# Reordered attention and mixer steps, stage results handed on by feature halves, first weights in two transfers

## The chip, the core and the metric

One kernel runs on one core of a Trainium2 chip. The metric is the device time of one launch in microseconds (us); lower is better. All weights are in HBM in float32 and are read once for each launch; the profile moves 414 MB.

## The reference

The input is x, 256 tokens by 1024 features, batch 1. It passes seven stages, each behind a root-mean-square norm and followed by a residual sum. Cut to what matters:

```
h = rms_norm(x);  u = h @ w_in + b_in;  u = a * sigmoid(gate)          # A: 31-tap causal depthwise convolution
x += silu(layer_norm(conv(u))) @ w_out + b_out
x += (silu(h @ w_gate) * (h @ w_up)) @ w_down                          # B: dense FFN, width 2816
k, v, f = rms_norm(x, kv_norm) @ w_kvf;  q = rms_norm(x, mix_norm) @ w_q   # C: 16 heads of 64
s = q k' / 8 + cumsum(log_sigmoid(f))[query] - cumsum(...)[key]        #    causal softmax, then @ v, then @ w_o
logits = h @ router_w + router_b; top 2 of 8 experts; softmax          # D: mixture of experts, each a swiglu
x = rms_norm(x, final_norm)
proj = rms_norm(x) @ w_in_2  ->  8 attention heads with a relative bias,  # F: mixer
        and 8 heads of a gated delta rule: 4-tap convolution, silu, q and k normalised per head,
        chunks of 64 tokens, unit triangular solves, a state carried across chunks,
        output normed per head, times silu(z)
x += rms_norm(concat(o_att, o_gdn) @ w_out_2)
x += rms_norm(relu(h @ w_up_2)**2 @ w_down_2)                          # G: MLP, width 4096
```

## The kernel before

**Tiling.** Tokens lie in two blocks of 128 (tb = 0, 1), features in eight blocks of 128 (k). A result of 256 x 1024 is four quarters (tb, nh): a token block by a half of 512 features. Every large product is made of three TensorE products in a fast float32 format: each operand is split into a high and a low part (`split`, L168: ScalarE copies the high part, VectorE subtracts it from the source), and high x high, high x low and low x high are added (`mm3`, L152). A weight chunk is a "raw" tile of 128 x 2048 (1 MB, one transfer on SP's queue, `wraw` L230) that is split in two halves of 128 x 1024 (`wload` L242). There are 4 raw slots and 6 slots each for high and low halves.

**Accumulators.** PSUM has eight banks of 128 x 512: four with the tag "mm" (projections, scores, transposed probabilities, small products) and four with the tag "acc" (the quarters of a result, transposes of a result, attention values). A step that asks for a bank waits until an instruction has read its last holder.

**Stages hand over through a feed.** `finish` (L470) runs the last contraction rows of a result quarter by quarter, in the order of `QUARTERS` (L468: both halves of token block 0, then those of block 1), adds the residual with VectorE, and calls `Feed.piece` (L371) for each quarter: four transposes on TensorE, then ScalarE and VectorE copy them as high and low parts, times the norm's gain. The next products have the features on the contraction axis. `lin_feat` and `lin_bank` (L269, L274) do all eight blocks of one output half, then of the other. `lin_first` (L286) does the first four blocks of both output halves, each in a bank of its own, then the last four. `Feed.R` (L451) spreads the norm's factor over a tile, by two products into a bank. `RouteFeed.piece` (L999) is the router's form: it keeps transposed copies and makes the logits from them.

**Order.** A planner orders the instructions of each engine from estimated durations. `tc.issue_after(last_pe[0])` forces what follows behind the last TensorE product; `seq` (L1431) does so for each step of a list, so that TensorE's queue has the order of that list. The forget attention (`forget_block`, L895) gives its steps by a string without forcing it: q, k, v are projection chunks of 256 columns, s the scores and softmax of a pair of heads (`att_scores`), o transposes and values of a pair (`att_values`, L876). The mixer (`mixer_block`, L1356) forces its steps with `seq`: qk_chunk, v_chunk, gdn_chunk and gate_chunk are projections, att_probs and att_out the two halves of its attention, then head sums and normalisation of q and k, gdn_scores, first_level, level and couple (the triangular solves), out_rows (w_out's first rows, put between), out_sums and spread (the output norm). In the expert stage, `down` and `transposes` (L1242 to L1268) of a chunk run behind the gate and up products of the next, and `scatter` (L1100) adds the last expert's rows back to the tokens.

Of the kernel before, what the change touches and what calls it, by code (L numbers as in the profile page):

```python
# [104 lines left out]
def kernel(ctx: ExitStack, tc: tile.TileContext, ins: dict, out: bass.AP):  # L105
# [74 lines left out]
    nc.sync.dma_start(cm[:, nmain:], ins["vecs"])  # L180
# [10 lines left out]

    def dw(j, c):
        return V("conv_w_dw", j * KD + c)
# [79 lines left out]

    def lin_bank(ps_, W, hT, nb):  # L274

        c = slice(nb * P, (nb + 1) * P)
        for k in range(KD):
# [84 lines left out]
    class Feed:  # L362
# [105 lines left out]
    QUARTERS = [(tb, nh) for tb in range(2) for nh in range(2)]  # L468

    def finish(acc, W, kt, first, done):  # L470
# [18 lines left out]
        for n, q in enumerate(QUARTERS):  # L489
# [142 lines left out]
    def conv_block(x, feed, nxt):  # L632
# [45 lines left out]
        def gate_pair(i, ps_):  # L678
            for c in range(2):
# [3 lines left out]
                stt(uv[cb][:, CPAD:], ps_[0][:, c * T:(c + 1) * T], V("conv_b_in", cb), sg, ALU.add, ALU.mult)  # L683
# [17 lines left out]
        for i in range(4):  # L701
            ps_ = [bank("pa"), bank("pg")]
            for j in range(2):
                lin_feat(ps_[j], W[j], hT)
# [58 lines left out]
    def conv_tail(x, cv, pst, ahead, raw, nxt):  # L763
# [43 lines left out]
    def ffn_block(x, feed, nxt):  # L807
# [16 lines left out]
        for c in range(n):  # L824
            sg, su = wk("fsg", 512), wk("fsu", 512)
            for key, w, o in (("g", wg, sg), ("u", wu, su)):
                W = feed.take((key, c), lambda: wcols(w, c))
                for nb in range(2):
                    ps_ = bank("p" + key)
                    lin_bank(ps_, W, hT, nb)  # L830
                    halves(o[:, nb * T:(nb + 1) * T], ps_)
                if key == "g":
# [14 lines left out]
    def att_scores(hp, qT, kT, add_bias, mask_of):  # L847


        res = []  # L850
        for j in range(2):
            h = 2 * hp + j
            s = slice(j * 64, (j + 1) * 64)
            ps_ = bank("sc")
            if add_bias:
                add_bias(ps_[:, 0:384], h)
            mm(ps_[:, 0:P], qT[s, 0:P], kT[s, 0:P], not add_bias, True)
            mm(ps_[:, P:P + T], qT[s, P:T], kT[s, :], not add_bias, True)
# [17 lines left out]
    def att_values(hp, probs, vtok, ohi, olo):  # L876

        po = bank("po", "acc")
        pTs = []
        for j in range(2):  # L880
            pt = bank("pt")
            for i in range(3):
                pe.transpose(pt[:, i * P:(i + 1) * P], probs[j][:, i * P:(i + 1) * P], ident)
# [3 lines left out]
        for j in range(2):  # L887
            s = slice(j * 64, (j + 1) * 64)
            vc = slice((2 * hp + j) * 64, (2 * hp + j + 1) * 64)
            mm(po[s, 0:T], vtok[0][:, vc], pTs[j][:, 0:T], True, False)  # L890
            mm(po[s, P:T], vtok[1][:, vc], pTs[j][:, T:384], False, True)
# [3 lines left out]
    def forget_block(x, feed, nxt):  # L895
# [16 lines left out]
        def forget_logits():  # L912
            fT = lin_small(ins["w_f"], 16, hkv, feed.R, -1.0)
# [28 lines left out]

        def values(hp):
# [4 lines left out]
        def k_chunk(i):  # L948
            ps_ = bank("pk")
            lin_feat(ps_, feed.take(("k", i), lambda: wcols(w_kvf, i)), hkv)  # L950
# [20 lines left out]
        nls = forget_logits()  # L971
        v_chunk(0)
        feed.rest()
        k_chunk(1)
        forget_gates(nls)
        for step in "q0 s0 s1 q1 o0 v1 o1 s2 s3 k2 o2 q2 o3 v2 s4 s5 k3 o4 q3 o5 s6 s7 v3 o6 o7".split():
            {"k": k_chunk, "q": q_chunk, "v": v_chunk, "s": scores, "o": values}[step[0]](int(step[1]))
# [9 lines left out]
    class RouteFeed(Feed):  # L987
# [11 lines left out]
        def piece(self, tb, half, x):  # L999
            if self.pl is None:  # L1000
                self.pl, self.xt = bank("pl"), []
            ps_ = bank("tr", "acc")
            for i in range(4):
                tr = pe.transpose(ps_[:, i * P:(i + 1) * P], x[:, half * 512 + i * P:half * 512 + (i + 1) * P], ident)
            last_pe[0] = tr.ins
            xt = wk("rt", 512)
            act.activation(xt, ps_, AF.Copy)
            self.xt.append(xt)
            if half == 1:
                self.stat(tb, x)  # L1010
            else:
                self.xh.append(b4("xh", F32R))
                self.xl.append(b4("xl", F32R))
# [3 lines left out]
            def logits(j):  # L1017
                for i in range(4):
                    k = j % 2 * 4 + i
                    mm(self.pl[:, j // 2 * NE:(j // 2 + 1) * NE], self.xt[j][:, i * P:(i + 1) * P],  # L1020
                       self.rw[:, k * NE:(k + 1) * NE], k == 0, k == KD - 1)

            if (tb, half) == (1, 0):
                logits(0)
            if (tb, half) == (1, 1):
                with tc.issue_after(tr.ins):
                    for j in range(1, 4):
                        logits(j)

    def moe_block(x, feed, nxt):  # L1030
# [69 lines left out]
        def scatter(acc, yhi, ylo, GT, gate, bk, after=None):  # L1100
# [4 lines left out]
            for tb in range(2):  # L1105
                s = slice(tb * P, (tb + 1) * P)
                for nh in range(2):
                    cc = slice(nh * 512, (nh + 1) * 512)
# [3 lines left out]
                    stt(x[tb][:, cc], ps_, gate(tb), x[tb][:, cc], ALU.mult, ALU.add)  # L1112
                    if after:
                        after(tb, nh, x[tb])
# [830 lines left out]
```

## Time and profile before

| | |
|---|---|
| median of 3 runs | 1684.16 us (1683.49 to 1686.7) |
| profiled execution | 1683.93 us, span 1681.8 us |
| mean granted TensorE clock | 0.983 |
| TensorE (PE) busy | 1605.4 us, 95% of the span |
| VectorE (DVE) busy | 1268.6 us, 75% |
| ScalarE (ACT) busy | 1042.2 us, 62% |
| GpSimd (POOL) busy | 74.3 us, 4% |
| DMA | 414.39 MB, mean 246 GB/s |

Busy shares are means over the whole span. The stages lie one behind another, in us from the start: convolution to 131, dense FFN to 320, forget attention to 449, router to 460, experts to 1257, scatter to 1266, mixer to 1490 (its attention to about 1355, the delta rule behind it), MLP to the end. A granted clock of 1.00 is 2.4 GHz, 0.50 is 1.2 GHz.

### The profile page before, as it was taken

To read this page: it belongs to the slowest core of one execution; us is meant where nothing else is said; L and a number is where in the kernel's file an instruction comes from. 1 tells how busy PE (TensorE), PEld (TensorE's weight loads), DVE (VectorE), ACT (ScalarE), POOL (GpSimd) and SP (SyncE) were. 2 spreads that over 40 slices of the span, in tenths; PEclk is the share of its full clock that TensorE was granted. 3 is DMA by queue.
4 is the path that set the end of the run, shared out by engine and by line. 5 is a ranking of instruction groups with operands and counts; after the bars stand their busy time and mean duration, and the time that the engine had idled before them with its cause. 6 is when DMAs were issued, how large, how long until landed. Compare 5 with 4: busy or idle time off the path is not lost. (4 is left out here: it accounts for less than half of the span.)

```text
span 1681.8 us, 25138 instructions
## 1 busy us (share of the span) xinstructions
PE 1605.4 (95%) x9788; PEld 1335.3 (79%) x9788; DVE 1268.6 (75%) x1795; ACT 1042.2 (62%) x1531; POOL 74.3 (4%) x119
## 2 busy tenths in 40 slices
PE   7999999999889999999999999999898898989998
PEld 6768888898778787778877788777667887878886
DVE  4467766776578899899988999988878765476665
ACT  4256555565467777777777877777666453355543
POOL 2400000000000000000000000001000000010001
PEclk9989999999999999999999999999999989999999
DMA  6655555445629899999999999999994440036551
GB/s 234 183 180 199 184 196 179 170 145 184 217 82 344 343 349 360 367 360 380 341 375 355 376 358 341 373 369 380 363 336 152 142 145 27 5 131 208 199 180 46
DMA packets 61582, 414.39 MB, mean 246 GB/s; under 512 B 7560, under 2 KB 7952, under 8 KB 14224
## 3 DMA queue, kind: packets, MB, share of 16 engines
q1 hardware_dynamic: 56448, 396.87, 64.5%
q0 software_dynamic: 3712, 11.65, 2.3%
q10 hardware_dynamic: 1296, 4.19, 0.6%
q8 instruction: 79, 1.29, 0.3%
q14 instruction: 47, 0.39, 0.1%
HBM read 406.77 MB, written 5.91 MB: 245 GB/s over the span
## 5 line engine op out<-in xcount | busy, mean ns | idle before, releaser
L158 DVE TENSOR_TENSOR wlo<-raw,whi 128x1024 fp32r<-128x1024 f32 x752 | 897.7, 1230 | 227.1 <-ACT whi L169 223.1
L169 ACT ACTIVATE whi<-raw 128x1024 fp32r<-128x1024 f32 x752 | 761.3, 1057 | 201.9 <-issue 42.8
L147 PE MATMUL pgu<-whi,xg 128*128 128x512 f32 x1408 | 459.5, 395 | 5.7 <-PEq L1131 4.5
L147 PEld LDWEIGHTS pgu<-whi,xg 128*128 128x128 f32 x1408 | 265.6, 189 | 60.7 <-PEq L1131 4.9
L147 PE MATMUL pgu<-wlo,xg 128*128 128x512 f32 x704 | 288.4, 410 | 5.6 <-DVE wlo L158 5.5
L147 PEld LDWEIGHTS pgu<-wlo,xg 128*128 128x128 f32 x704 | 132.6, 188 | 49.5 <-DVE wlo L158 25.4
L147 PE MATMUL pu<-h,whi 128*128 128x512 f32 (+1 forms) x448 | 153.2, 388 | 0.5 <-DVE h L161 0.5
L147 PE MATMUL acc<-wlo,mhi 128*128 128x512 f32 x352 | 137.8, 392 | 1.0 <-DVE wlo L158 1.0
L147 PE MATMUL acc<-whi,mlo 128*128 128x512 f32 x352 | 137.1, 390 | 0.0
L147 PE MATMUL acc<-whi,mhi 128*128 128x512 f32 x352 | 124.6, 390 | 1.4 <-ACT whi L169 1.4
L147 PE MATMUL pu<-h,wlo 128*128 128x256 f32 x432 | 121.0, 280 | 0.0
L147 PEld LDWEIGHTS pu<-h,whi 128*128 128x128 f32 x448 | 83.1, 188 | 19.1 <-DVE h L161 0.7
L1097 ACT ACTIVATE msg<-pgu,rse 128x256 f32<-128x256 f32 x88 | 41.7, 474 | 74.5 <-PE pgu L147 74.5
L147 PE MATMUL acc<-whi,flo 128*128 128x512 f32 x216 | 85.1, 394 | 0.0
L147 PE MATMUL acc<-whi,fhi 128*128 128x512 f32 x216 | 85.0, 393 | 0.0
L147 PE MATMUL acc<-wlo,fhi 128*128 128x512 f32 x216 | 84.8, 393 | 0.0
L147 PEld LDWEIGHTS pu<-h,wlo 128*128 128x128 f32 x432 | 81.6, 189 | 0.6
L147 PEld LDWEIGHTS acc<-wlo,mhi 128*128 128x128 f32 x352 | 66.1, 188 | 17.6 <-DVE wlo L158 3.7
L147 PEld LDWEIGHTS acc<-whi,mhi 128*128 128x128 f32 x352 | 65.9, 188 | 15.7 <-ACT whi L169 2.0
L147 PEld LDWEIGHTS acc<-whi,mlo 128*128 128x128 f32 x352 | 66.1, 188 | 13.1
L169 ACT ACTIVATE mhi<-mpt 128x256 fp32r<-128x256 f32 x88 | 33.8, 384 | 60.5 <-PE mpt L1245 60.5
L147 PE MATMUL pg<-h,whi 128*128 128x512 f32 x176 | 62.3, 396 | 0.8 <-DVE h L161 0.8
(424 smaller groups left out, 2452.6 us busy)
## 6 DMA issues: line engine op xcount, KB each, us to landing
raw<-in_moe_w_gu_dram SPq DMA_DIRECT2D x172, 1024.0 KB, 6.9
raw<-in_moe_w_down_dram SPq DMA_DIRECT2D x86, 1024.0 KB, 6.7
raw<-in_w_up_dram SPq DMA_DIRECT2D x16, 1024.0 KB, 5.0
raw<-in_w_down_dram SPq DMA_DIRECT2D x16, 1024.0 KB, 4.9
raw<-in_w_in_dram SPq DMA_DIRECT2D x14, 1024.0 KB, 4.9
raw<-in_ffn_w_gate_dram SPq DMA_DIRECT2D x11, 1024.0 KB, 4.9
raw<-in_ffn_w_up_dram SPq DMA_DIRECT2D x11, 1024.0 KB, 5.0
raw<-in_ffn_w_down_dram SPq DMA_DIRECT2D x11, 1024.0 KB, 4.9
```

Of the source, the lines that this page charges most:

```text
L147: last_pe[0] = pe.matmul(o, l, r, start=start, stop=stop, skip_group_check=True).ins
L158: return (eng or dve).tensor_tensor(out=o, in0=a, in1=b, op=op)
L169: return act.activation(hi, src, AF.Copy), tt(lo, src, f(hi), ALU.subtract, eng)
L1097: act.activation(sg, pgu[:, 0:256], AF.Silu, scale=r)
```

## The change

- **Start.** The vector table is loaded from ScalarE's queue instead of SP's; its columns for the 31-tap weights (248, read by nothing) are dropped. The first weight chunk comes as two transfers of half the width. The first convolution products use `lin_first`.
- **Convolution's tail.** SiLU writes the high part directly, and runs a second time in float32 for the low part.
- **Stage results.** `QUARTERS` goes by feature half: (0,0), (1,0), (0,1), (1,1). The pieces of the first half are given under the third quarter's products; the others after the fourth. The first products of the FFN, of the attention and of the mixer do the contraction blocks of the first half first (`lin_first`, and `lin_bank` with `ks`). The factor's bank is then an "acc" bank in the mixer; `R_late` puts its products at the place in the queue where it is called. The router makes all its logits behind the last piece. The scatter of the last expert goes by feature half, and its pieces are given behind the last sum.
- **Attention.** `att_values` is parted: `att_turn` transposes the probabilities, `att_values` multiplies. Scores and values of the two heads of a pair alternate. In the forget attention the gate logits go behind the first v chunk, q0 before the gates, and the string of steps has t steps and is forced.
- **Experts.** Of the last expert's last chunk but one, the second half of the down products goes behind the last transposes, and the end is forced.
- **Mixer.** New lists for `seq`; the second gate chunk goes before the normalisation; `out_sums` has the squares as the stationary side and gives 128 x 16 sums; `spread` multiplies a broadcast column by the identity.

The core of the diff ("..." for lines left out):

```diff
-    nc.sync.dma_start(cm[:, nmain:], ins["vecs"])
+    nc.scalar.dma_start(cm[:, nmain:], ins["vecs"])
...
+    def lin_bank(ps_, W, hT, nb, ks=range(KD)):
...
+        def R_late(self):
+            with tc.issue_after(last_pe[0]):
+                return self.R()
...
-                    self.bc["ps"] = bank("rb")
+                    self.bc["ps"] = bank("rb", "acc" if self.stats_late else "mm")
...
-    QUARTERS = [(tb, nh) for tb in range(2) for nh in range(2)]
+    QUARTERS = [(tb, nh) for nh in range(2) for tb in range(2)]
...
-        for n, q in enumerate(QUARTERS):
+        for n, q in enumerate(QUARTERS if give else sorted(QUARTERS)):
             with tc.issue_after(last_pe[0]):
                 quarter(*q)
             taken[q] = take(*q)
-            if n == 2:
-                with tc.issue_after(last_pe[0]):
-                    give_after((0, 0), (1, 0))
-        for q in QUARTERS[1:]:
+            if give and n == 2:
+                for g in QUARTERS[:2]:
+                    with tc.issue_after(last_pe[0]):
+                        give_after(g, q)
+        for q in QUARTERS[2:]:
             with tc.issue_after(last_pe[0]):
                 give_after(q, (1, 1))
...
-            act.activation(cv[cb], cv[cb], AF.Silu, scale=V("conv_ln_g", cb), bias=V("conv_ln_b", cb))
-            h_, l_ = split(hi[cb // 4][:, o], lo[cb // 4][:, o], cv[cb])
+            h_ = act.activation(hi[cb // 4][:, o], cv[cb], AF.Silu, **sb)
+            act.activation(cv[cb], cv[cb], AF.Silu, **sb)
+            l_ = tt(lo[cb // 4][:, o], cv[cb], f(hi[cb // 4][:, o]), ALU.subtract)
...
+                if (key, c) == ("g", 0):
+                    for ks in (range(KD // 2), range(KD // 2, KD)):
+                        for nb in range(2):
+                            lin_bank(pss[nb], W, hT, nb, ks)
...
+        pss, rows = [bank("sc") for _ in range(2)], [slice(j * 64, (j + 1) * 64) for j in range(2)]
...
+        for j, s in enumerate(rows):
+            mm(pss[j][:, 0:P], qT[s, 0:P], kT[s, 0:P], not add_bias, True)
+        for j, s in enumerate(rows):
+            mm(pss[j][:, P:P + T], qT[s, P:T], kT[s, :], not add_bias, True)
...
+    def att_values(hp, pTs, vtok, ohi, olo):
+        po = bank("po", "acc")
+        for w in range(2):
+            for j in range(2):
...
+                mm(po[s, w * P:T], vtok[w][:, vc], pTs[j][:, w * T:T + w * P], w == 0, w == 1)
...
+        small = lin_small_mm(ins["w_f"], 16, hkv, feed.R, -1.0)
         v_chunk(0)
+        nls = forget_logits(small)
         feed.rest()
         k_chunk(1)
+        q_chunk(0)
         forget_gates(nls)
-        for step in "q0 s0 s1 q1 o0 v1 o1 s2 s3 k2 o2 q2 o3 v2 s4 s5 k3 o4 q3 o5 s6 s7 v3 o6 o7".split():
...
+        for step in ("v1 s0 s1 q1 t0 k2 o0 t1 s2 q2 o1 t2 s3 v2 o2 t3 s4 k3 o3 t4 s5 q3 o4 t5 s6 s7 v3 o5 t6 t7 o6 o7"
+                     .split()):
+            with tc.issue_after(last_pe[0]):
+                steps[step[0]](int(step[1]))
...
-            if (tb, half) == (1, 0):
-                logits(0)
...
+                with tc.issue_after(last_pe[0]):
+                    for q in sorted(self.xt):
+                        logits(*q)
...
+            if after:
+                for q in QUARTERS:
+                    with tc.issue_after(varop[0]):
+                        after(*q, x[q[0]])
...
+                if pend and (e, c) == (NE - 1, NCH - 1):
+                    with tc.issue_after(last_pe[0]):
+                        down(pend, (0,))
+                    before = pend
...
+        with tc.issue_after(last_pe[0]):
+            transposes(pend)
+        with tc.issue_after(last_pe[0]):
+            down(before, (1,))
...
+            if (m, i) == (0, 0):
+                return lin_first("paq", chunk(0), hT)
...
         qk_out(1, 0, first[1])
+        seq(lambda: gdn_chunk(2))
...
+        with tc.issue_after(last_pe[0]):
+            for tb in range(2):
+                last_pe[0] = pe.transpose(pab[:, tb * 16:(tb + 1) * 16], ...
...
+        seq(lambda: att_probs(0))
...
-        seq(lambda: gdn_chunk(2), lambda: att_probs(0), lambda: v_chunk(0))
+        seq(lambda: v_chunk(0), lambda: att_probs(1), lambda: gdn_chunk(3))
...
-        seq(lambda: att_probs(1), lambda: gdn_chunk(3), att_out, lambda: qk_chunk(0, 1), att_out, lambda: qk_chunk(1, 1),
-            lambda: att_probs(2), lambda: gdn_chunk(0), lambda: att_probs(3), lambda: v_chunk(1), att_out,
-            lambda: gdn_chunk(1), att_out)
+        seq(att_t, lambda: qk_chunk(0, 1), att_out, att_t, lambda: qk_chunk(1, 1), att_out, lambda: gdn_chunk(0),
+            lambda: att_probs(2), lambda: gdn_chunk(1), lambda: att_probs(3), lambda: v_chunk(1), att_t)
...
-        seq(lambda: gdn_chunk(4), lambda: gdn_chunk(5))
+        seq(lambda: gdn_chunk(4), att_out, att_t, lambda: gdn_chunk(5))
...
-        seq(head_sums)
+        seq(att_out, head_sums)
...
-        seq(lambda: gate_chunk(0), normalize)
+        seq(lambda: gate_chunk(0), lambda: gate_chunk(1), normalize)
...
-        seq(v_tokens, lambda: gdn_scores(0), lambda: gate_chunk(1))
...
-        seq(lambda: gdn_scores(1), lambda: out_rows(0, 0), lambda: first_level(0), lambda: out_rows(1, 0),
-            lambda: gdn_scores(2), lambda: level(0, 2), lambda: out_rows(2, 0), lambda: gdn_scores(3))
+        seq(lambda: gdn_scores(0), v_tokens, lambda: out_rows(0, 0), lambda: gdn_scores(1), lambda: out_rows(1, 0),
+            lambda: out_rows(2, 0), lambda: first_level(0), lambda: gdn_scores(2), lambda: level(0, 2),
+            lambda: out_rows(3, 0), lambda: gdn_scores(3))
...
-        seq(lambda: out_rows(3, 0), lambda: level(0, 4), lambda: first_level(1))
+        seq(lambda: level(0, 4), lambda: first_level(1))
...
-            for b in range(4):
-                mm(pn2[:8, :T], v3(C("ind"), 16)[:, b, 0:8], osq[:, b * T:(b + 1) * T], b == 0, b == 3)
+            for tb in range(2):
+                for b in range(4):
+                    mm(pn2[:, tb * 8 + 2 * b:tb * 8 + 2 * b + 2], osq[:, b * T + tb * P:b * T + (tb + 1) * P],
+                       v3(C("ind"), 16)[:, 0, 0:2], True, True)
...
         dve.reciprocal(out=rn2, in_=rn2)
-        rn2 = two_parts(rn2, 8)
...
-                mm(pbs[b // 2][:, b % 2 * T:(b % 2 + 1) * T], hsel[0:40, b * P:(b + 1) * P], rn2, True, True)
+                for tb in range(2):
+                    o = b % 2 * T + tb * P
+                    for j in range(2):
+                        c = tb * 8 + 2 * b + j
+                        mm(pbs[b // 2][j * 64:(j + 1) * 64, o:o + P], rn2[:, c:c + 1].to_broadcast([P, 64]), ident, True, True)
...
+            def halved():
+                raw = wpool.tile([P, 2048], F32, tag="raw", name=nm("raw"), bufs=RAW_BUFS)
+                parts = [raw[:, c:c + CV] for c in range(0, 2048, CV)]
+                for i, t in enumerate(parts):
+                    nc.sync.dma_start(t, ins["conv_w_in"][0][:, i * CV:(i + 1) * CV])
+                return wload(None, 256, None, parts)
...
-         ("kv_norm", 8), ("final_norm", 8), ("pre_mix_norm_2", 8), ("pre_mlp_norm_2", 8), ("conv_w_dw", 248), ("conv_w_2", 48),
+         ("kv_norm", 8), ("final_norm", 8), ("pre_mix_norm_2", 8), ("pre_mlp_norm_2", 8), ("conv_w_2", 48),
```

## Rows read from the trace of the kernel before

**Rows 1.** Stretches: window, us, busy by engine (x instructions), granted clock, DMA share, GB/s.

```profile
320.00:360.00 40.00, 36.30 (x299) 34.81 (x297) 33.87 (x98) 28.15 (x68) 3.92 (x4) 1.00 0.44 159
360.00:450.00 90.00, 88.85 (x627) 78.31 (x625) 52.46 (x140) 47.97 (x105) 0.14 (x1) 1.00 0.57 199
1284.00:1380.00 96.00, 84.28 (x645) 77.34 (x644) 68.11 (x176) 50.07 (x90) 2.13 (x6) 0.96 0.39 137
```

**Rows 2.** TensorE's waits by releaser: us in total, times, longest us.

```profile
PE po L147 <- ACT pT L885: 5.0, 6, 1.8
...
PE pbc L147 <- DVE parts L158: 3.4, 1, 3.4
PE pos L147 <- DVE sel L165: 3.4, 1, 3.4
PE pab L1449 <- DVE smo L161: 3.0, 1, 3.0
...
PE paq L147 <- DVE hlo L161: 2.1, 1, 2.1
...
PE pi L147 <- DVE N L161: 1.5, 1, 1.5
PE tr L150 <- DVE x L158: 1.5, 2, 0.7
PE sc L147 <- DVE ak L158: 1.5, 1, 1.5
...
PE pf L916 <- DVE smo L161: 1.2, 1, 1.2
PE sc L147 <- DVE qT L158: 1.1, 1, 1.1
...
PE pg L147 <- DVE h L161: 0.8, 1, 0.8
...
PE pk L147 <- DVE hlo L161: 0.7, 1, 0.7
```

**Rows 3.** Stretches of half the granted clock, columns as in rows 1.

```profile
1345.90:1349.30 3.40, 3.40 (x17) 3.40 (x17) 0.42 (x1) 3.39 (x5) 0.00 (x0) 0.50 0.44 176
1380.00:1386.80 6.80, 6.34 (x28) 5.81 (x30) 4.42 (x8) 1.95 (x5) 0.00 (x0) 0.50 0.46 157
1400.50:1407.30 6.80, 6.40 (x47) 5.11 (x49) 1.01 (x3) 1.12 (x4) 0.00 (x0) 0.50 0.01 2
```

**Rows 4.** The chain that ended last: start us, us, engine, tile, line, instructions.

```profile
1312.42 5.85 PE paq L147 x47
...
1345.78 7.33 PE pqkv L147 x47
...
1461.83 1.90 PE pog L147 x32
```

**Rows 5.** ScalarE's timeline at the start: start us, us, instruction, [idle before, releaser].

```profile
9.95 2.00 ACT L169 ACTIVATE whi<-raw 128x1024 fp32r<-128x1024 f32 x2 [2.46 <-DMA raw<-in_conv_w_in_dram]
```

**Rows 6.** TensorE's timeline, seven places, columns as in rows 5.

```profile
87.30 1.48 PE L147 MATMUL pv<-cm,sq 128*128 128x1 f32 x12
...
370.30 0.94 PE L147 MATMUL po<-pT,v 128*64 128x256 f32 x8
...
1257.75 0.73 PE L147 MATMUL acc<-whi,mhi 128*128 128x512 f32 x2 [1.42 <-ACT whi L169]
...
1294.66 0.93 PE L147 MATMUL sc<-ak,aq 64*128 64x128 f32 x8
...
1311.19 1.24 PE L147 MATMUL po<-pT,av 128*64 128x256 f32 x8 [0.76 <-ACT pT L885]
...
1470.01 1.89 PE L147 MATMUL pn<-osq,cm 128*8 128x256 f32 x8
...
1475.28 0.93 PE L147 MATMUL pob<-parts,hsel 40*128 40x256 f32 x4 [1.79 <-DVE parts L158]
```

**Rows 7.** The page's costliest group: busy us, mean ns of one, idle before.

```profile
L158 DVE TENSOR_TENSOR wlo<-raw,whi 128x1024 fp32r<-128x1024 f32 x752 | 897.7, 1230 | 227.1 <-ACT whi L169 223.1
```

More of the change, by code (lines that the diff above doesn't have):

```diff
@@ L272, in lin_feat @@
             lin_part(ps_[:, nb * T:(nb + 1) * T], W, hT, nb, range(KD))
-    def lin_bank(ps_, W, hT, nb):
+    def lin_bank(ps_, W, hT, nb, ks=range(KD)):
         c = slice(nb * P, (nb + 1) * P)
-        for k in range(KD):
+        for k in ks:
             mm(ps_, W[0][k][:, c], hT[2][k], k == 0, False)
@@ L701, in conv_block @@
         for i in range(4):
-            ps_ = [bank("pa"), bank("pg")]
-            for j in range(2):
-                lin_feat(ps_[j], W[j], hT)
+            if i == 0:
+                ps_ = [lin_first("pa", W[0], hT), bank("pg")]
+                lin_feat(ps_[1], W[1], hT)
+            else:
+                ps_ = [bank("pa"), bank("pg")]
+                for j in range(2):
+                    lin_feat(ps_[j], W[j], hT)
             if i < 3:
@@ L827, in ffn_block @@
                 W = feed.take((key, c), lambda: wcols(w, c))
-                for nb in range(2):
[L829 to L832, printed above, removed]
+                pss = [bank("p" + key) for _ in range(2)]
+                if (key, c) == ("g", 0):
+                    for ks in (range(KD // 2), range(KD // 2, KD)):
+                        for nb in range(2):
+                            lin_bank(pss[nb], W, hT, nb, ks)
+                for nb in range(2):
+                    if (key, c) != ("g", 0):
+                        lin_bank(pss[nb], W, hT, nb)
+                    halves(o[:, nb * T:(nb + 1) * T], pss[nb])
+                if key == "u":
+                    if c == 0:
+                        feed.R_late()
                     tt(v3(sg, T), v3(sg, T), feed.R2(), ALU.mult)
@@ L874, in att_scores, with att_turn @@
         return res
-    def att_values(hp, probs, vtok, ohi, olo):
-        po = bank("po", "acc")
+    def att_turn(probs):
         pTs = []
@@ L948, in k_chunk @@
         def k_chunk(i):
+            W = feed.take(("k", i), lambda: wcols(w_kvf, i))
+            if i == 0:
+                for nb, ps_ in enumerate(lin_first("pk", W, hkv)):
+                    tt(half(kTt, i)[:, nb * T:(nb + 1) * T], ps_, feed.R_late(), ALU.mult)
+                return
             ps_ = bank("pk")
-            lin_feat(ps_, feed.take(("k", i), lambda: wcols(w_kvf, i)), hkv)
+            lin_feat(ps_, W, hkv)
             tt(v3(half(kTt, i), T), v3(ps_, T), feed.R2(), ALU.mult)
@@ L1104, in scatter @@
                 split(yhi[:, cc], ylo[:, cc], acc[nh])
[L1105 to L1108, printed above, removed]
+            for nh in range(2):
+                cc = slice(nh * 512, (nh + 1) * 512)
+                for tb in range(2):
+                    s = slice(tb * P, (tb + 1) * P)
                     ps_ = bk()
@@ L1244, in transposes, with down @@
             for j in range(2):
-                pe.transpose(pt[:, j * P:(j + 1) * P], p["sg"][:, j * P:(j + 1) * P], ident)
+                transpose(pt[:, j * P:(j + 1) * P], p["sg"][:, j * P:(j + 1) * P])
             p["hi"], p["lo"] = wk("mhi", 256, F32R), wk("mlo", 256, F32R)
             split(p["hi"], p["lo"], pt[:, :256])
-        def down(p):
+        def down(p, nhs=range(2)):
             e, c = p["e"], p["c"]
             J = jobs[e]
-            Wd = feed.take(("d", e, c), lambda: wrows(moe_d[e], c))
-            for nh in range(2):
+            Wd = p.get("W") or feed.take(("d", e, c), lambda: wrows(moe_d[e], c))
+            p["W"] = Wd
+            for nh in nhs:
                 for j in range(2):
@@ L1441, in mixer_block @@
         abT = lin_small_out(*first[2])
-        qk_out(0, 0, first[0])
+        for nb in range(2):
+            tt(aq[:, nb * T:(nb + 1) * T], first[0][nb], feed.R(0.125), ALU.mult)
         qk_out(1, 0, first[1])
+        seq(lambda: gdn_chunk(2))
+        x = feed.base()
         dtb = bc_small("dt_bias_2")
@@ L1447, in mixer_block @@
         pab = bank("pab")
-        for tb in range(2):
-            pe.transpose(pab[:, tb * 16:(tb + 1) * 16], abT[:16, tb * P:(tb + 1) * P], ident[0:16, 0:16])
+        with tc.issue_after(last_pe[0]):
+            for tb in range(2):
+                last_pe[0] = pe.transpose(pab[:, tb * 16:(tb + 1) * 16], abT[:16, tb * P:(tb + 1) * P],
+                                          ident[0:16, 0:16]).ins
         ya = sm("ya", 16, bufs=1)
```

95 lines of the change are left out of this document (46 added, 49 removed).

## The prediction

> **What bounds the kernel now.** I read the stage table first. In the two stretches that hold the forget attention TensorE is busy 36.3 of 40 us and 88.9 of 90, VectorE 33.9 of 40 and 52.5 of 90; in the front of the mixer TensorE is busy 84.3 of 96 and VectorE 68.1 [rows 1]. So TensorE sets the pace, and what a stage can give back is TensorE's idle time and its slow stretches; VectorE is close behind only between 320 and 360 us. Second I read TensorE's waits: each row is one dependence on which it stood still [rows 2]. Third the granted clock: behind several of these waits it reads 0.50, 1.2 instead of 2.4 GHz, for some microseconds [rows 3]. What that costs is seen in the chain of waits: 47 products of 128x256 take 5.85 us normally and 7.33 us where 3.4 us of them lie in the stretch at 1345.9 [rows 4]. That is 1.48 us lost for 3.4, so about 3.0 for a stretch of 6.8. The expert stage between 465 and 1180 is touched only at its last two chunks.
>
> **The change part by part** (gains negative, in us).
>
> *Start.* ScalarE waits 2.46 us for the first weight block, starts its split at 9.95, and splits two halves for 2.00 us; only then come the copies of the transposed input that the first products need [rows 5]. After: 0.5 MB lands instead of 1 MB, without the 248 unread columns ahead of it (124 KB, 0.12 MB), so the first half can be split before the transposes are through, and only the second is left to collide. One of two splits moves out of the way, 1.0 us, and the load itself is earlier. The trace has no such split load: bounds 0 (the second half comes at the same time and stands ahead again) and -2.46 (the whole wait goes). I take -1.5. What is late next is the transposes. The vector table now goes out on ScalarE's queue, ahead of its own first loads: SP is relieved of one issue, and ScalarE was waiting for the input anyway, so 0. A rule of the Trainium skill speaks against the cut: "DMA: Bandwidth & Descriptors", section Bandwidth, says that transfers of 1 MiB or more are wanted for 75% of the peak. No row of mine shows two halves against a whole; by that rule the term would be nearer to 0, inside the bounds.
>
> *Convolution.* SiLU writes the high part directly, and is run a second time for the low part: as many ScalarE instructions, the first one earlier. Between 0 and -0.4; taken as 0.
>
> *Stage borders to the dense FFN and to the attention.* Quarters of the result now finish by feature half, the first half's transposes go under the fourth quarter, and the next products take their first four contraction blocks on that half alone. Before, TensorE stood twice for the residual sum (1.5 together) and once at each border for the low part of the transposed input (0.8 on pg, 0.7 on pk) [rows 2]. That is 3.0. The first-half products, 24 instructions of 0.12 (5.85 / 47 [rows 4]), last 2.9 us and cover the second half's copies. If the planner puts the last transposes ahead of them, the wait of 0.7 for the last sum stays at each border. Bounds -3.0 and -1.5; taken -2.8.
>
> *Forget attention.* Three edits. (a) Order: the gate logits wait behind v0, q0 stands before the gates: the waits of pf (1.2) and of the first scores for q (1.1) get 5.9 us of products in front of them and go. Transposes of the probabilities are parted from the value products by at least one other step: of 5.0 us of waits on pT, 4.0 lie in the mixer, 1.0 here [rows 2]. Together -3.3. (b) Value products of the two heads alternate. A pair of heads took 1.24 us in its old order; where two heads happened to run alongside each other it took 0.94 [rows 6]. 0.3 for each pair, and seven of the eight pairs here were in the slow form: -2.1. (c) Score products alternate too, but those already run alongside: eight instructions in 0.93 us [rows 6]. So 0. Against this: every step is now queued on TensorE behind the step before. A pair of scores takes two of the four banks at once and a transposing step two more, so a step that waits for a bank holds everything behind it. One such wait is worth at most a split of 1.23 us on VectorE ahead of the instruction that frees the bank [rows 7]. I count +1.0 for all. And between 320 and 360 VectorE has only 6 us to spare [rows 1], so a TensorE that runs 4 us faster there will meet late splits: +1.5. Sum -2.9; bounds -5.4 and +3.
>
> *Router.* Two pieces instead of three are left when the last quarter ends, and ScalarE's last square sum ends sooner; the wait of 3.4 us for the routing on VectorE stays [rows 2]. All 16 logit products now stand at the end instead of 12. Bounds 0 and -1.5; taken -0.9.
>
> *Last experts and scatter.* Half of the last but one down product is put behind the last transposes, 6 products of 0.23. The wait behind these transposes was 1.42, and it was for a weight split [rows 6], which is queued on ScalarE behind the copy of the transposes; both move up a little: -0.6, bounds 0 and -1.42. Scattering by feature half lets the mixer's first products start once the first half is turned; the wait was 2.1 [rows 2]. The remaining part is the copies of two pieces: -1.5, bounds -0.5 and -2.1.
>
> *Mixer.* pab waited 3.0 us; now a projection stands in front. But the first q product now holds two banks, k one, the small product one: four of four, so the projection needs the very instruction (smo) that pab waited for. I take -1.0 of the 3.0; bounds 0 and -3.0. The rest of the waits on pT (4.0) and the scores' wait for ak (1.5) get whole projections between: -5.5. Four value pairs: -1.2. The second gate projection (5.9 us) goes in front of the normalisation, whose wait was 3.4 [rows 2]: -3.4. With these waits the slow stretches behind them go: 3.4 us at 1345.9 (-1.5) and 6.8 us at 1380 (-3.0) [rows 3]. In exchange the first delta-rule scores stand directly behind the normalisation, and need two of its four multiplies and three of its banks: +1.2; v_tokens wants a bank that these scores hold: +0.3. Two output rows instead of one cover the scores' wait N (1.5): -1.3; but the row that stood between the last scores and the second first_level is gone from there: +0.7. The slow stretch at 1400.5, behind that wait, and a like one at 1475.6 (3.0 each): I count half of each, -3.0.
>
> The output norm: old sums are 8 instructions in 1.89; the new ones are 8 products of two columns, each two passes, 16 instructions. Twelve one-column ones took 1.48, 0.12 each [rows 6], so 1.9: no gain. The Trainium skill, "TensorEngine Tiling (Array Packing)", section Instruction Overhead, says about 60 cycles for a product that short; 16 would take 0.4 us and the sum would be 1.5 lower. The row, five times as long, decides for me. Root and reciprocal then work on 128x16 instead of 8x256 and the two-part split goes: the wait of 1.79 ahead of pob goes [rows 6]. The spread becomes 32 instructions of 128 columns by 64 rows, which in pog took 1.90 [rows 4], against 4 in 0.93, and the first gated block is ready later by half of that. Net -1.3; bounds +1 and -2.4. Mixer: -1.0-5.5-1.2-3.4-4.5+1.5-0.6-3.0-1.3 = -19.0, and +1.0 for VectorE, which would be busy 80% instead of 71%: -18.0. Bounds -27 and -7.
>
> **Sum.** -1.5-2.8-2.9-0.9-2.1-18.0 = -28.2. The profiled execution is 1683.93, its span 1681.8; the median of the runs is 0.23 higher. 1683.9 - 28.2 = 1655.7, so 1656.
>
> **Rivals.** *New waits take half.* The waits removed are a few microseconds each and TensorE's order is now fixed, so what was late by 0.8 is soon late elsewhere by 0.5; the clock still falls behind them. For: VectorE at 85% from 320 to 360, and the four banks. Against: the projections put in front are 5.9 us long, the waits 0.8 to 3.4. Half of the sum: 1670. *All of it lands.* The mixer keeps the full clock to its end (-3.0 more), pab goes (-2.0), the attention has no new waits (-2.5), the rest at its far bound (-4): 1644. Against: four banks, and small products, behind which the clock fell before. *Slower: the fixed queue stands for banks.* Some 30 steps in the attention and 16 in the mixer are queued strictly; if nearly each waits one split of 1.23, 46 x 1.23 = 57 us go in and 28 come out: 1712. It decides from 23 such waits on. For: scores, transposes and products share four banks. Against: before, the same pairs s0 s1 q1 ran without any wait on a bank in [rows 2]. *No effect:* the planner had the order already; 1684. Against: the waits of [rows 2] are all there.
>
> **How the numbers follow.** Forecast 60%, half 20%, all 11%, no effect 5%, slower 4%. The range: the forecast's own is 1648 to 1664; it reaches to 1643 and 1674, which leaves out half of the far case, "no effect" and "slower". 0.2% is 3.4 us, about what the measurement can tell: faster by more 0.91, within 0.05, slower 0.04.
>
> **What would show it.** Right: no wait of TensorE over 0.5 us on pT, pbc, pf, ak; the borders without waits on the residual sum; value pairs at 0.9; pob without its wait; no 0.50 at the places of 1345.9 and 1380. Wrong: waits of score or projection products on VectorE's reduces (banks); pqkv standing behind smo for 3 us; sums of two columns at 0.4 us; VectorE over 90% between 320 and 355; a gain below 14.

## The result and the profile after

The changed kernel takes 1664.51 us, median of 4 runs (1659.15 to 1668.35), against 1684.18 before (1683.49 to 1686.7). The ratio is 0.9878, interval [0.9849, 0.9908]. The profiled execution is 1664.85, its span 1662.8, 19.0 us less than before.

The table cuts both kernels at the first product of the same kind in each stage, in us between the marks. The kernel before has three profiles (two of them runs below), the changed one two.

| from, to | before | changed |
|---|---|---|
| start to the layer norm's spread product | 102.8, 102.0, 101.9 | 104.0, 104.1 |
| to the FFN's first product | 31.0, 31.0, 31.0 | 29.2, 29.4 |
| to the attention's first k product | 187.7, 187.6, 187.7 | 187.4, 187.5 |
| to the routing | 136.7, 136.9, 136.9 | 131.2, 131.7 |
| to the last gate-and-up product of the experts | 794.6, 798.2, 794.3 | 796.5, 796.0 |
| to the scatter | 9.0, 9.8, 9.0 | 8.6, 8.6 |
| to the mixer's small product | 18.7, 20.6, 18.7 | 17.0, 17.0 |
| to the MLP's first product | 213.9, 208.5, 213.9 | 200.7, 203.3 |
| to the end | 187.4, 187.5, 187.4 | 188.1, 188.2 |

So the gain is the mixer's 13.2 us (first profile against first; 5.1 to 13.2 over all pairs of these profiles), the attention's 5.5, and about 4 at the borders. The start loses 1.2, or some 2 over all profiles, as start_ea below shows. The experts' stretch is 1.9 longer, but it scatters by itself. The last stretch is 0.8 longer; no run explains that.

TensorE's waits after, columns as in [rows 2]:

```profile
PE tr L437 <- DVE xn L165: 12.1, 2, 11.4
...
PE pi L147 <- DVE Y L158: 3.5, 9, 1.2
PE pqkv L147 <- DVE smo L161: 3.1, 1, 3.1
PE pos L147 <- DVE sel L165: 2.8, 1, 2.8
PE pgc L147 <- DVE gg L161: 2.7, 1, 2.7
...
PE pi L147 <- DVE Vi L158: 1.2, 2, 0.6
...
PE pi L147 <- ACT Y L1694: 1.0, 2, 0.8
PE pi L147 <- ACT dc L1615: 0.9, 2, 0.4
...
PE pk L147 <- DVE hlo L161: 0.6, 2, 0.4
PE pbc L147 <- DVE zs L158: 0.5, 1, 0.5
...
PE po L147 <- ACT pT L903: 0.3, 1, 0.3
...
PE pg L147 <- DVE h L161: 0.2, 1, 0.2
```

Before, four waits that [rows 2] leaves out read:

```profile
PE tr L435 <- DVE xn L165: 8.5, 1, 8.5
...
PE pi L147 <- DVE Y L158: 2.4, 8, 1.2
...
PE pi L147 <- DVE Vi L158: 1.6, 2, 1.0
...
PE pi L147 <- ACT Y L1633: 0.9, 2, 0.8
```

Of [rows 2] the waits on pT (5.0), pbc (3.4), ak, qT, pf, N and the residual sums are gone or under 1 us. N's has only moved: the products of the triangular solves (pi) waited 6.4 us in all before, with the 1.5 for N, and wait 6.6 now. Another has only changed its name: pab stood 3.0 us for smo, the scaled result of the small product, and now pqkv stands 3.1 for it. One is new, the decay products (pgc) wait 2.7 for gg, the logarithms of the decays. One is longer: the first transposes wait for the normalised x until 11.4 instead of 8.5.

The stretches that answer to [rows 1] and [rows 3], same columns, show a TensorE with less idle time in both attentions, and four half-clock stretches of 3.4 us from the mixer's start to the MLP's:

```profile
320.00:360.00 40.00, 38.87 (x320) 37.39 (x319) 32.26 (x85) 28.20 (x59) 2.82 (x4) 1.00 0.44 160
360.00:442.00 82.00, 81.55 (x602) 71.44 (x601) 52.70 (x155) 47.61 (x113) 0.00 (x0) 1.00 0.60 218
1277.00:1372.00 95.00, 88.66 (x697) 81.80 (x695) 70.49 (x180) 51.43 (x91) 1.91 (x6) 0.96 0.43 149
1282.00:1285.40 3.40, 3.40 (x18) 3.40 (x17) 0.94 (x1) 0.00 (x0) 0.00 (x0) 0.50 0.77 260
1305.90:1309.30 3.40, 3.40 (x17) 2.80 (x17) 3.16 (x8) 1.13 (x3) 0.11 (x1) 0.50 0.31 130
1401.50:1404.90 3.40, 3.40 (x66) 3.40 (x68) 1.02 (x3) 2.57 (x5) 0.00 (x0) 0.50 0.02 5
1473.20:1476.60 3.40, 3.40 (x18) 3.40 (x17) 3.17 (x14) 3.27 (x13) 0.00 (x0) 0.50 0.00 0
```

The slow stretches at 1345.9 and 1380 of [rows 3] have no counterpart in this profile. That at 1282.0 lies behind the wait on smo, and that at 1305.9 behind the wait on gg.

TensorE's timeline after, at three places of [rows 6]:

```profile
370.67 0.87 PE L147 MATMUL po<-pT,v 128*64 128x256 f32 x8
...
1453.34 2.02 PE L147 MATMUL pn<-cm,osq 128*128 128x2 f32 x16
...
1456.78 1.97 PE L147 MATMUL pob<-cm,rn 128*64 128x128 f32 x32
1458.91 0.50 PE L147 MATMUL acc<-whi,ohi 128*128 128x512 f32 x1 [0.16 <-ACT ohi L169]
```

A pair of value products takes 0.87 instead of 1.24, the sums of two columns cost 2.02 for 16, the spread 1.97, and pob has no wait ahead of it.

VectorE's timeline at the start, before and then after, shows the loss there (start us, us, instruction, idle before):

```profile
7.74 1.62 DVE L165 TENSOR_SCALAR xn<-x,rstd 128x1024 f32<-128x1024 f32 x2
11.04 2.36 DVE L158 TENSOR_TENSOR wlo<-raw,whi 128x1024 fp32r<-128x1024 f32 x2 [1.68 <-ACT whi L169]
```

```profile
9.47 1.23 DVE L158 TENSOR_TENSOR wlo<-raw,whi 128x1024 fp32r<-128x1024 f32 x1 [1.10 <-ACT whi L169]
10.62 0.75 DVE L165 TENSOR_SCALAR xn<-x,rstd 128x1024 f32<-128x1024 f32 x1
11.28 1.22 DVE L158 TENSOR_TENSOR wlo<-raw,whi 128x1024 fp32r<-128x1024 f32 x1
12.41 0.74 DVE L165 TENSOR_SCALAR xn<-x,rstd 128x1024 f32<-128x1024 f32 x1
```

Before, both multiplies that normalise x came first. Now a low part of the weights stands ahead of each. The weights land as early as was wished, and the planner, which orders VectorE's queue, puts them first; x, which every product needs, comes 2.9 us later.

### The profile page after: what moved, and what is told of

The parts are those of the page before. It is cut to its first block, busy times and chain, and to the rows that moved or that the text cites. A ratio compares the mean times of both kernels' runs of the same rounds, so it can differ in the third digit from the quotient of the medians.

```text
span 1662.8 us, 25206 instructions
## 1 busy us (share of the span) xinstructions
PE 1599.2 (96%) x9824; PEld 1329.8 (80%) x9824; DVE 1264.4 (76%) x1796; ACT 1043.1 (63%) x1530; POOL 72.4 (4%) x118
## 5 line engine op out<-in xcount | busy, mean ns | idle before, releaser
L158 DVE TENSOR_TENSOR wlo<-raw,whi 128x1024 fp32r<-128x1024 f32 x752 | 897.5, 1231 | 217.8 <-ACT whi L169 213.9
```

The source lines that it names most:

```text
L158: return (eng or dve).tensor_tensor(out=o, in0=a, in1=b, op=op)
```

## Experiments

Each kernel is the changed one with the edit shown. Times are medians; the ratio is to the kernel before on the same chip. Because executions of one kernel differ by several us, the verdicts rest on the stretches that an edit touches. By the ratios alone only fix4 lies clear below the changed kernel (0.9849 to 0.9915 by the intervals of its two measurements) and only old_mixer clear above both; the intervals of the others overlap with it.

**The changed kernel again.**

> The changed kernel itself, once more, as the measure for the others. If its runs of 1659 to 1668 us are one kernel's scatter, its profile differs from the first one by some us in stretches where both have the same instructions (the experts, 738.3 us, or the clock); if the scatter is one of place, it stays within 1 us of 1664.5. Ratio to the kernel before 0.986 to 0.990.

1667.5 us (1658.8 to 1671.6), ratio 0.9887 [0.9859, 0.9915]. Its profile is 3.1 us longer than the first, 2.7 of it in the mixer, where it has 17.0 us of half clock up to the output norm against 10.2. The experts took 787.9 in both. So the difference between these two profiles is mostly the clock's; what sets the ends of the range was not profiled.

**VectorE's order at the start** (start_order), and with it **the exponential moved** (start_ea).

```diff
...
-                return wload(None, 256, None, parts)
+                return lambda: wload(None, 256, None, parts, lo_after=fd.last_xn)   # low parts behind xn
...                                                                               # start_ea only:
-        act.activation(ea, alog, AF.Exp)
+        with tc.issue_after(old_exp):        # the forget attention's last exponential
+            act.activation(ea, alog, AF.Exp)
```

> The first weight chunk still comes in two halves, but the low parts of its split go behind the two VectorE multiplies that normalise x. Theory 1 (the loss of 1.2 us at the start comes from VectorE's order: the first low part stands ahead of the normalised x, which starts at 10.6 instead of 7.7): the first transposes start at 8 to 9 us, the first product at 12 to 13.5 instead of 15.0, and the stage ends 1.5 to 3 us earlier than in the changed kernel. Rival (the half transfers or the vector table on the other queue delay x and the weights themselves): the first product stays after 14.5 and the time within 0.5 us of the changed kernel's.

> As start_order, and the exponential of A_log is ordered behind the forget attention's exponentials on ScalarE. Theory 1 (with the low parts moved, the copies of the transposed input stood behind that exponential, which waited for its small table until 12.3): the first copy starts at 11 to 11.5 instead of 12.4 and the first product at 12.5 to 13 instead of 13.9; the convolution's end comes 1 us earlier than in start_order. Rival (the transposes themselves or the second token block of x are late): the first product stays at 13.6 to 14.

start_order: 1664.2 us, ratio 0.988 [0.9851, 0.9909]. The transposes start at 8.9 instead of 11.4, the first product at 13.9 instead of 15.0, less than theory 1 had, and the layer norm is reached 1.3 us earlier. ScalarE's timeline in start_order shows what was late next:

```profile
9.67 1.06 ACT L255 ACTIVATE whi<-raw 128x1024 fp32r<-128x1024 f32 x1 [0.25 <-DMA raw<-in_conv_w_in_dram]
12.32 0.21 ACT L1522 ACTIVATE ea<-smalls 128x8 f32<-128x8 f32 x1 [1.59 <-DMA smalls<-in_smalls_dram]
12.43 0.82 ACT L443 ACTIVATE hhi<-tr,cm 128x256 fp32r<-128x256 f32 x2
```

An exponential that only the mixer needs waits 1.59 for its table, and the first copy of the transposed input stands directly behind it. In the changed kernel itself this cost nothing yet: there the copy waits until 13.73 for the transposes, 1.07 behind the exponential. With the exponential moved too (start_ea: 1660.1 us, ratio 0.9846 [0.9821, 0.9872]) the same engine reads:

```profile
9.79 1.06 ACT L255 ACTIVATE whi<-raw 128x1024 fp32r<-128x1024 f32 x1 [0.25 <-DMA raw<-in_conv_w_in_dram]
10.75 0.82 ACT L443 ACTIVATE hhi<-tr,cm 128x256 fp32r<-128x256 f32 x2
```

The first product is at 12.2. The third weight chunk's first product, before at 27.9 and in the changed kernel at 29.2, is at 27.8 in start_order and 26.8 in start_ea. So the two queues' order was worth 1.4 and 1.0, and with both right the start gains 1.1 on the first profile of the kernel before. Over all profiles this product is at 27.1 to 27.9 in the kernel before, at 28.7 to 29.5 in the seven kernels with the changed start unaltered, and at 26.8 and 27.0 in start_ea and fix4: the change lost 0.7 to 2.4 us there, and the repair gains 0.1 to 1.1. The layer norm is a poorer mark, because half clock ahead of it differs: the same seven reach it at 101.8 to 105.9. The four of them with 3.4 us of half clock, which all three profiles of before have, reach it at 104.0 to 104.8, against 101.9 to 102.8. The forecast of a convolution's end 1 us earlier than in start_order failed: it came 0.8 later, with a half-clock stretch of 6.8 at 88.0 instead of 3.4 at 89.2.

**The first weights whole** (start_whole).

```diff
-            fd.early = {("in", 0): halved}
+            fd.early = {("in", 0): lambda: wcols(ins["conv_w_in"], 0)}
```

> The first weight chunk in one transfer again; the vector table stays small and on ScalarE's queue. In this kernel VectorE's queue has the first normalised x, then both low parts of the first weights, then the second normalised x. Theory 1 (the order on VectorE decides): the first transposes start at 8 to 9 us, those of the second token block only after both low parts, at 12.5 to 13.5, and the first product at 14 to 15.5. Rival (the halves as such cost the time): the first product at 13.4 as before the change.

One execution: 1666.9 us. The transposes start at 8.5, the second token block's only behind both low parts at 13.4, the first product is at 14.7, the third chunk's at 32.0. This is theory 1's order of things. ScalarE splits the whole block from 9.19 to 11.20; with halves, in the changed kernel, it starts at 8.38 and ends at 10.73. So the two transfers did bring the weights earlier. That the third chunk is 2.8 later than with halves was forecast by neither; the planner had also put g's products between a's, so the halves alone are not priced by it.

**The small product's bank** (small_acc).

```diff
...
-        ps_ = bank("psm")
+        ps_ = bank("psm", tag)          # tag="acc" for the mixer's call
```

> The bank of the mixer's small product (the 16 columns of a and b) is taken from the accumulators' four instead of the projections' four. Theory 1 (the projection put in front of pab waits for a bank that the small product holds until smo has read it): the wait of 3.1 us of pqkv on smo goes to under 1 us, the slow clock behind it (1282.0 to 1285.4) too, and the mixer is 3 to 4.5 us shorter. Rival (it waits for the spread factor or for the residual's sums, which every reader of the first banks needs): the wait stays at 2 us or more under another name, gain below 1 us.

1661.7 us, ratio 0.9854 [0.9829, 0.9878]. The wait on smo is gone and so is the slow stretch behind it. From the small product to the head sums it takes 77.9 us instead of 82.8 and 84.3. Theory 1 holds for this stretch; behind it 3.5 us come back (below). From the small product to the MLP it is 199.0, 1.7 less than in the changed kernel's first profile, where theory 1 had 3 to 4.5; seven profiles with the mixer's list unaltered (the changed kernel's two, the three of the start, old_forget and heads_serial) have 198.6 to 203.3, so this gain alone is not clear of their scatter.

**The decay products later** (decays_late).

```diff
-        seq(decays)
+        seq(att_t, lambda: qk_chunk(0, 1), decays)
...
-        seq(att_t, lambda: qk_chunk(0, 1), att_out, att_t, ...
+        seq(att_out, att_t, ...
```

> The decay products on gg go one transposing step and one q projection later in the forced list of the mixer. Theory 1 (TensorE stood 2.7 us only because these five products stand at the head of a fixed list while gg is late on VectorE): the wait on gg goes, the half clock at 1305.9 with it, and the mixer is 2.7 to 4.2 us shorter. Rival (VectorE is late with everything there, and the next step that needs it waits as long): a wait of 1.5 us or more on pT or on a projection's bank appears in its place, gain below 1.2 us.

1658.6 us, ratio 0.985 [0.9825, 0.9874]. The wait on gg is gone, nothing over 1.0 us took its place ahead of the head sums, and the same stretch takes 78.2. Behind it both kernels have 6.8 us of half clock at the normalisation, which the changed kernel's first profile had not (its second has 3.4), and lose 3.4 to 3.5 us of the gain again. The mixer to the MLP is 198.7 here, 2.0 less than in that first profile, where theory 1 had 2.7 to 4.2. The stretches of small_acc and of decays_late:

```profile
1369.50:1376.30 6.80, 6.70 (x29) 5.89 (x29) 4.23 (x8) 1.84 (x5) 0.00 (x0) 0.50 0.44 143
```

```profile
1374.40:1381.20 6.80, 6.80 (x29) 5.94 (x28) 3.65 (x7) 2.42 (x7) 0.00 (x0) 0.50 0.46 154
```

**All four repairs** (fix4).

> Four repairs together: low parts of the first split behind the normalised x, the exponential of A_log (ScalarE waited 1.6 to 1.7 us for its table at the start with the copies of the transposed input behind it) behind the forget attention, the mixer's small product in the accumulators' banks, the decay products one step later. Theory 1 (each wait is a price of its own): first product at 12.5 to 13 us instead of 15.0; from the mixer's small product to the head sums 72 to 74.5 us, where one repair alone gave 77.9 and 78.2 and the changed kernel 82.8 and 84.3; in all 6 to 9 us under the changed kernel of the same job, 1655 to 1660. Rival (the granted clock falls at another place of the mixer when it does not fall at one): the mixer up to the across product stays at 168 us or more, with 10 us of half clock in it, and the gain in all is 2 to 4 us.

1652.7 us (1651.6 to 1655.5), ratio 0.9806 [0.9786, 0.9826]: faster than both kernels. The small product to the head sums takes 73.3: 82.8 less 4.9 and 4.7 is 73.2, so the two waits with the clock behind them add up. The rival is right in one point: the stretch from the normalisation to the product of the step `across`, late in the delta rule, is 74.7 instead of 71.3, with 13.6 us of half clock. But from the small product to `across` it takes 163.3 instead of 169.4, where the rival had 168 or more, and to the MLP 193.9 instead of 200.7, clear below the seven unaltered mixers. TensorE's waits left there, columns as in [rows 2], the longest in total first:

```profile
PE pi L147 <- DVE Y L158: 3.5, 9, 1.2
PE tr L150 <- DVE x L161: 2.1, 1, 2.1
...
PE pbc L147 <- DVE zs L158: 0.6, 1, 0.6
```

**The mixer as before** (old_mixer): the whole function of the kernel before, on the changed helpers, with `att_values(h_, att_turn(pr), ...)` in one step.

> The changed kernel with the mixer's whole text as before (its lists, its output norm, its first q product in one bank), on the changed helpers, with transposes and values of a pair directly behind one another. Theory 1 (14 of the 19 us come from the mixer's lists and its output norm): the time goes back by 11 to 15 us, and the waits of the value products on the transposed probabilities (4.0), on the normalisation (3.4) and on ak (1.5) are there again. Rival (much of it comes from the helpers, the handing on by halves and the alternating heads, which stay): it goes back by 5 to 9.

1678.2 us, ratio 0.9955 [0.9938, 0.9972]: 13.7 above the changed kernel's first median, 10.7 above its second. The mixer, from the small product to the MLP, takes 213.2, against 198.6 to 203.3 in the seven. The waits are back:

```profile
PE po L147 <- ACT pT L903: 4.0, 4, 1.8
PE pab L1494 <- DVE smo L161: 3.5, 1, 3.5
PE pbc L147 <- DVE parts L158: 3.4, 1, 3.4
...
PE pob L147 <- DVE parts L158: 1.8, 1, 1.8
...
PE pi L147 <- DVE N L161: 1.5, 1, 1.5
PE sc L147 <- DVE ak L158: 1.5, 1, 1.5
```

**The forget attention's old order** (old_forget).

```diff
...
-        for step in ("v1 s0 s1 q1 t0 k2 o0 t1 s2 q2 o1 ...").split():
-            with tc.issue_after(last_pe[0]):
-                steps[step[0]](int(step[1]))
+        for step in "q0 s0 s1 q1 o0 v1 o1 s2 s3 k2 o2 ...".split():
+            if step[0] == "o":
+                turn(int(step[1]))
+            steps[step[0]](int(step[1]))
```

> The changed kernel with the forget attention's steps in their old order, not forced, transposes directly ahead of the values, the gate logits ahead of the first v chunk and q0 behind the gates; heads still alternate. Theory 1 (the waits on pf, q and the transposed probabilities were worth 3.3 us there and nothing took their place): from the first k product to the routing 133.5 to 135.5 us instead of 131.2 to 131.7, the time 2 to 4 us up. Rival (most of the gain came from the alternating heads and the hand-over by halves): under 133 us, the time up by under 1.5.

1672.8 us, ratio 0.9923 [0.991, 0.9937]. From the first k product to the routing 137.1 us, all that the stage had gained, and more than theory 1 expected. The waits on qT, pf and pT are back (1.1, 1.0, 1.0), and the pairs of value products are slow again, five of eight by the full 0.38, although the code alternates the heads:

```profile
359.38 1.24 PE L147 MATMUL po<-pT,v 128*64 128x256 f32 x8
```

How much of the stage's gain is the order's, the forcing's or the step's between transposes and values, this run does not part.

**One head behind the other** (heads_serial).

```diff
-        for w in range(2):
-            for j in range(2):
+        for j in range(2):
+            for w in range(2):
```

> The changed kernel with the value products of one head behind those of the other again; all else as changed. Theory 1 (two heads run alongside each other only when their products alternate): each of 12 pairs takes 1.17 us from its first product to what follows instead of 0.80, 4.4 us in all, and the time goes up by 3 to 5. Rival (what is saved there is waited for behind it, on the next projection's weights or banks): the pairs take 1.17, and the time goes up by under 1.5.

1661.9 us, ratio 0.9854 [0.9836, 0.9872], no slower. Both theories failed on the pairs, which stay as in the changed kernel, ten of twelve fast:

```profile
371.00 0.88 PE L147 MATMUL po<-pT,v 128*64 128x256 f32 x8
```

In either order the first products of the two heads start 0.02 us apart or less in these ten pairs. In the kernel before and in old_forget the second head's starts 0.37 later than the first's in the slow pairs. There the transposes stand directly ahead, TensorE waits for the first head's copy, and the second copy is not done. The traces show it pair by pair: wherever the second copy ends behind the first head's start, by 0.02 to 0.33 us, the second head starts 0.05 to 0.06 us behind that end. (Left out is the last pair of these two kernels, whose second head stands behind other products.) The two slow pairs of the changed kernel, o6 and o7, stand close behind their transposes too, and show the same 0.05. So what makes two heads run alongside each other is that both copies are ready, by the step put between, and not the alternation.

**The kernel before, twice more.**

> The kernel before, once more, for its scatter. In the nine profiles of kernels with the change so far the experts' stretch, from the first to the last gate-and-up product, took 787.5 to 791.6 us, in the one profile of before 786.2; the instructions there are the same but for the last chunk. Theory 1 (this is scatter of the weight stream): 787 to 792 here. Rival (a stage that begins earlier is given part of it back, the weights being no earlier): 785.5 to 786.8 again.

> The same a third time. Theory 1: the experts' stretch differs from the two others by over 1 us; the half-clock stretches of the mixer, 20.4 us up to the output norm in the first profile, differ by 3.4 or more from one profile to another. Rival: within 0.6 us and 0 of the first.

1684.3 and 1682.9 us. From the first to the last gate-and-up product 790.0 and 786.1, after 786.2. The stretch scatters by 4 us in the kernel before as well; in eleven profiles with the change it was 787.5 to 792.5. So theory 1 of the first of these two holds for one profile and its rival for the other. Whether an earlier start lengthens the stretch by a us or two these runs don't settle. before_third has the mixer's half-clock stretches of the first profile, before_again has 10.2 instead of 20.4 from the small product to the output norm, and that part is 4.4 us shorter there.

## Why the prediction was right, and where it was not

The direction, the range and the place of the gain were right; the size was 19.7 us where 28.2 were forecast, just beyond the forecast's own range of 1648 to 1664. By its steps, first profile against first:

- **Borders, attention, router** (forecast -6.6): -7.5, right in the sum, partly by luck: the two borders gave -2.1 of -2.8, attention and router -5.5 of -3.8. Most waits went as read, and VectorE and the banks, for which +2.5 was set aside, took nothing: but for the routing's own 2.8, no wait of TensorE there is over 0.9. The border of the convolution was about right at -1.9. That of the attention gave 0.2: its wait on the low part stayed, 0.6 instead of 0.7.
- **Value pairs** (-2.1 and -1.2): right in size, 0.37 instead of 0.3 for each pair that became fast, wrong in cause. The prediction gave the gain to the alternation of the heads; heads_serial and old_forget give it to the step between transposes and values.
- **Last experts and scatter** (-2.1): -2.1.
- **Start** (-1.5): this step failed, +1.2, some +2 over all profiles. It named ScalarE's collision and the transposes as next, and did not ask what else the earlier weights would be put in front of: VectorE's multiplies of x. The bounds ended at 0, and the truth lay beyond them. start_order shows the cause, start_ea the second queue behind it.
- **Mixer** (-18.0): -13.2. The waits on pT and ak went in full, that on the normalisation but for 0.5. Four terms failed. pab (-1.0) gave nothing: the projection waits 3.1 for the bank that the text named, the whole old wait, and small_acc shows it; the text had this among its signs of being wrong. N (-1.3 and +0.7) gave nothing either: the solves' products wait 6.6 in all instead of 6.4. The new wait on gg (2.7, and the half clock behind it, together 4.7 by decays_late) was not in the sum: five products on a late operand now stand at the head of a fixed list. The new waits that were in it (+1.5, at the first delta scores and v_tokens) did not come, nor does VectorE's +1.0 show: it is busy 70.5 of 95 us in the mixer's front, 74% and not 80%.
- **Slow stretches** (-7.5): 27.2 us of half clock from the mixer's start to the MLP's became 13.6, at 0.44 us lost for each some -6.0. But this is partly the draw of one execution: the four profiles with the old mixer's steps have 17.0 to 27.2, the seven with the new ones 6.8 to 20.4.
- **Output norm** (-1.3): the sums cost 1.88 to the next product, the spread 2.13 with its 0.16 of wait, the two waits of 1.8 and 0.6 are 0.2. From the sums to the first gated block it is 5.6 instead of 6.8 us, -1.2. The row decided rightly: 0.12 us for each of the 16 instructions. The short price of the Trainium skill ("TensorEngine Tiling (Array Packing)", section Instruction Overhead), about 60 cycles, is not what this trace shows.
- **The rival "new waits take half"** (1670) is nearer to the measured time, 5.5 us above it, than the forecast, 8.8 below. Its mechanism is there: two waits at the fixed queue and one order on VectorE took about a third of the 28.2. fix4, which removes them, ends at 1652.7, where the forecast with 1655.7 and the rival "all of it lands" with 1644 lie on both sides.

## What to carry to other kernels

When an operand is made to arrive earlier, ask on every engine what it will now be put in front of; here 2.9 us of x were paid for weights that nothing could use yet. When a list is forced, look at each step for its latest operand and for the bank that it takes: a step with a late one holds up all behind it, and moving it by one step or to other banks gave 4.7 and 4.9 us up to the head sums, of which half clock behind it took back 3.4 to 3.5, no more when both were done together. Put a step between a transpose pair and the products that use both halves, and the halves run alongside each other.

## What the runs showed of the hardware

Two chains of products on different 64-column halves of TensorE overlapped whatever their order in the queue, if both operands were there at the start (0.87 us against 1.24); if not, the second chain started 0.05 to 0.06 us behind its operand, alongside the first. The same mixer text ran with 6.8, 10.2, 13.6 and 17.0 us of half clock between the scatter and the output norm, in profiles whose waits on smo, on gg and at the normalisation agree to 0.1 us; a single profile's slow stretches are no fixed price. Executions of the changed kernel differ by 13 us (1658.8 to 1671.6).
